# Attention heads: the 16 meta keys kept as 96 stacked rows, and one product in place of three

## The chip, the core and the metric

The kernel runs on one core of a Trainium2 chip. The metric is the device time of one execution in microseconds; the median of several runs counts. TensorE (PE) multiplies and transposes, VectorE (DVE) and ScalarE (ACT) do everything element by element, SyncE (SP) issues the loads. Each engine works through its own instructions in a fixed order and waits on the others by semaphores.

## The reference, cut to what matters

512 frames with 16 learned meta tokens ahead of them (528 rows of 1024) pass through two layers. Layer 0 has two kinds of attention side by side, four differential heads and eight forgetting ("fox") heads; layer 1 is multi-scale retention. An MLP follows each. For every attention head, scores become probabilities, and the probabilities are multiplied by the values:

```
p_a = softmax(where(chunk_vis, s_a, -inf))
p_diff = p_a[:, :, 0] - lam * p_a[:, :, 1]
o_a = einsum('bhqk,bhkd->bhqd', p_diff, va)      # 4 heads, 128 value columns
...
p_b = softmax(where(frame_vis, s_b, -inf))
o_b = einsum('bhqk,bhkd->bhqd', p_b, vb)         # 8 heads, 64 value columns
```

The sum over k runs over 16 meta keys and 512 frame keys. The change is in how the 16 meta keys enter that sum. All of it is float32.

## The kernel before

**Products in three passes.** A float32 operand is split in a high part `h` (ACT rounds it into the format that TensorE takes at full rate) and a low part `l` (DVE: source minus `h`). A product is three matmuls, `h*h + h*l + l*h`, in one PSUM bank. `split` makes such a pair from a bank. With only 16 rows to sum over, a matmul still streams all its 512 columns, three times.

**Stacked rows.** The same three terms can be summed over rows instead. `split_stack` gets a bank with 96 rows, six copies of 16 rows, and makes one tile in which one pair of the copies holds the low part and the others the high part. If the other operand has high and low parts in matching rows, one matmul over 96 rows gives all three terms. Layer 1 does so already: there `hm`, the six-fold copy of the meta rows of the hidden state, makes the values' meta block as 96 rows, and `mix_values` has a branch for it.

**A head of attention in layer 0.** The loop runs over four differential heads and then over eight fox heads. For head h the code issues, in this order:

- `diff_scores` or `fox_scores`: for four blocks of 128 query rows the scores (PSUM tile `s_ps`), with bias and minimum on DVE and the exponential on ACT, into the probability tiles `e`. Between the blocks stand the "filler" matmuls (PSUM tile `mm` for the next head's projections, `v_ps` for the fox heads' values).
- `diff_mix` or `fox_mix` of the head before (PSUM tile `o_ps`): `mix_values` multiplies values by probabilities in 12 matmuls over frame keys and three over the 16 meta keys.
- the scores between the meta rows themselves (`sm_ps`).
- `turn`: the probabilities are transposed on TensorE (PSUM tiles `t_ps`). Ten transposes of 128x128 fill three banks, four transposes of the 16 meta columns (`e[:, :16]`) a fourth. ACT and DVE split the banks: two of them at once into `turned` (in the last two heads one by one), the half-filled third and the meta bank into pairs `s`.

**The meta rows as queries** are few enough for one softmax over many heads: `meta_turn` transposes those 16x16 probabilities (`mt_ps`), `diff_meta_mix` and `fox_meta_mix` multiply them (`mo_ps`), three matmuls of 16 columns for each head.

**Order.** From the first head to the last, the flag `pe.on` chains every matmul and transpose to the one before it, so TensorE runs in the order of the code. ACT, DVE and the queue SP are put in order by the compiler's scheduler when the kernel is built. Tiles called `s`, `st`, `copies`, `e` and `turned` come from one pool of 43 buffers in SBUF, `s_ps`, `o_ps`, `v_ps` and the single `t_ps` from four PSUM banks, `mm` and the double `t_ps` from two pairs of banks.

Nearly all matmuls are recorded under line 156 and all transposes under line 159 (the helper that keeps the order), `split` under 352 (ACT) and 353 (DVE), `split_stack` under 416 and 418, the weights' split under 228 and 229.

Of the kernel before, what the change touches and what calls it, by code (L numbers as in the profile page):

```python
# [14 lines left out]
P = 128  # L15
# [3 lines left out]
META = 16  # L19
# [102 lines left out]
def kernel(  # L122
# [51 lines left out]
    def two(dt=F32, name="u"):  # L174
        t = both(dt, name)
        return t[:, 0, :], t[:, 1, :]
# [16 lines left out]
    def f(t):  # L193
        return t.bitcast(F32)
# [182 lines left out]
    for j in range(KT // 2):  # L377
        raw = both(F32, "xf")
        for i in range(2):
            load(raw[:, i, :], x[2 * j + i])  # L380
        for i in range(2):
            pair = both(F32R, "s")
            xs.append(split(raw[:, i, :], dst=(pair[:, 0, :], pair[:, 1, :])))
            act.copy(out=hm[:, 2 * j + i, :4 * META].rearrange("p (a c n) -> p a c n", a=2, c=2),
                     in_=f(pair)[:, :, :META].rearrange("p a (o n) -> p a o n", o=1).broadcast_to([P, 2, 2, META]))
        if j < 3:
            prepare(load)

# [25 lines left out]
    def split_stack(src, low, n):  # L414
        t = two(F32R, "st")[0]
        act.copy(out=t[:STACK, :n], in_=src)
        rows = slice(32 * low, 32 * low + 32)
        dve.tensor_tensor(out=t[rows, :n], in0=src[rows, :], in1=f(t)[rows, :n], op=ALU.subtract)
        return t
# [11 lines left out]
    def value_split(ps, t, n):  # L431
        if t < 4:
            return split(ps, n=512)
        if n == STACK:
            return split_stack(ps[:n, :], 2, 512)
        s = two(F32, "vm")[0][:32, :512]
        act.copy(out=s, in_=ps[32:64, :])
        dve.tensor_tensor(out=s, in0=s, in1=ps[:32, :], op=ALU.add)
        return split(s[:META], rows=slice(0, META), n=512)

    def value_block(xs, wts, t, n=4 * META):
        ps = bank("v_ps")
        for k in range(KT):
            for i in range(3 if t < 4 else 2):
                value_part(ps, xs, k, t, wts[k // 2], n, i)
        return value_split(ps, t, n)

    def value_streamed(xs):
        accs = [bank("v_ps") for _ in range(4)] + [two_banks("vm_ps")[:, 0, :]]
        for k in range(KT):  # L450
            if k % 2 == 0:
                wt = weights("B", ahead=3)
            order = [(t, i) for t in range(5) for i in range(3 if t < 4 else 2)]
            for t, i in order:
                value_part(accs[t], xs, k, t, wt, 4 * META, i)
        return [value_split(accs[t], t, 4 * META) for t in range(5)]

    va = value_streamed(xs)
    load_constants()
# [95 lines left out]
    def meta_scores(q, k, rows, fox, slot, into):  # L555
# [6 lines left out]
            pe.matmul(ps[:META, :META], lhsT=lhs, rhs=rhs, start=j == 0, stop=j == len(ops) - 1)  # L562
        dve.tensor_tensor(out=into[:, slot % 8, :], in0=ps[:META, :META], in1=mb_sb[:, slot, :], op=ALU.add)

    def turn(ps_list, wide=True):
        banks = [[(0, i) for i in range(4)], [(1, 1), (1, 2), (1, 3), (3, 3)], [(2, 2), (2, 3)]]

        def flip(ps, blocks):
            for c, (j, i) in enumerate(blocks):
                pe.transpose(out=ps[:, P * c:P * c + P], in_=ps_list[i][:, META + P * j:META + P * j + P],  # L570
                             identity=ident)
        turned = []
        if wide:
            ps = two_banks("t_ps")
            h, l = (both(F32R, "turned")[:, :, :512] for _ in range(2))
            for b in range(2):
                flip(ps[:, b, :], banks[b])
            act.copy(out=h, in_=ps)
            dve.tensor_tensor(out=l, in0=ps, in1=f(h), op=ALU.subtract)
            turned = [(h[:, b, :], l[:, b, :]) for b in range(2)]  # L580
        for blocks in banks[len(turned):]:
            ps = bank("t_ps")
            flip(ps, blocks)
            turned.append(split(ps, n=P * len(blocks)))
        ps = bank("t_ps")
        for i in range(4):
            pe.transpose(out=ps[:META, P * i:P * i + P], in_=ps_list[i][:, :META], identity=ident)
        turned.append(split(ps[:META, :512], rows=slice(0, META), n=512))
        return turned

    def mix_values(turned, v, vc0, ps):
        spans = [(0, 0, P, 0, 512, 0), (1, 1, P, 0, 384, 128), (2, 2, P, 0, 256, 256), (1, 3, P, 384, 128, 384),
                 (3, 4, META, 0, 512, 0)]
        stacked = not isinstance(v[4], tuple)
        if stacked:
            spans = spans[:4]
        for s, (src, blk, rows, s0, n, o0) in enumerate(spans):
            for i, (a, b) in enumerate(PASSES):
                pe.matmul(ps[:, o0:o0 + n], lhsT=v[blk][a][:rows, vc0:vc0 + P], rhs=turned[src][b][:rows, s0:s0 + n],
                          start=s == 0 and i == 0, stop=s == 4 and i == 2)  # L600
        if stacked:
            pe.matmul(ps, lhsT=v[4][:STACK, vc0:vc0 + P], rhs=turned[3][:STACK, :512], start=False, stop=True)

    os_ = [None] * KT
    od_t = [both(F32, "od") for _ in range(2)]
# [43 lines left out]

    def meta_turn(p, n):  # L650
        ps = bank("mt_ps")
        for i in range(n):
            pe.transpose(out=ps[:META, META * i:META * i + META], in_=p[:, i, :], identity=ident[:META, :META])
        return split(ps[:META, :META * n], rows=slice(0, META), n=META * n)

    def diff_meta_probs():
        meta_softmax(sm_d, 8)
# [6 lines left out]
    def diff_meta_mix(pt):  # L664
        ps = bank("mo_ps")
        for h in range(4):
            for i, (a, b) in enumerate(PASSES):
                pe.matmul(ps[:, META * h:META * h + META], lhsT=va[4][a][:META, P * h:P * h + P],
                          rhs=pt[b][:META, META * h:META * h + META], start=i == 0, stop=i == 2)
        for j in range(2):  # L670
            act.copy(out=od_t[j][:, :, :META],
                     in_=ps[:, 2 * META * j:2 * META * j + 2 * META].rearrange("p (a b) -> p a b", a=2))
# [95 lines left out]
    def fox_meta_mix(h0, h1, pt):  # L768
        ps = bank("mo_ps")
        for h in range(h0, h1):  # L770
            c = META * (h - h0)
            for i, (a, b) in enumerate(PASSES):
                pe.matmul(ps[:, c:c + META], lhsT=vb[4][a][:META, P * (h // 2):P * (h // 2) + P],
                          rhs=pt[b][:META, c:c + META], start=i == 0, stop=i == 2)
        for h in range(h0, h1):
            rows = slice(64 * (h % 2), 64 * (h % 2) + 64)
            dh, dl = os_[4 + h // 2]
            src = ps[rows, META * (h - h0):META * (h - h0) + META]
            act.copy(out=dh[rows, :META], in_=src)
            dve.tensor_tensor(out=dl[rows, :META], in0=src, in1=f(dh)[rows, :META], op=ALU.subtract)  # L780
# [490 lines left out]
    def ret_start(norm):  # L1271
        dst = [two(F32R, "qk") for _ in range(4)]
        aw = [weights("A") for _ in range(4)]
        bw = [weights("B") for _ in range(4)]
        v = [None] * 5

        for t in range(4):
            span = (META, HALF - META) if t < 2 else H1
            split_span(early_highs(aw[t], hs, span, None if t else norm), span, dst=dst[t])
        step(norm)  # L1280
        v[0] = value_block(hs, bw, 0, STACK)
        v[4] = value_block(hs, bw, 4, STACK)
        step(norm)
        for t in range(4):
            split_span(early_highs(aw[t], hs, H2), H2, dst=dst[t])
        return dst[:2], dst[2:], v, bw
# [83 lines left out]
    for h in range(RET_HEADS):  # L1370
        if h:
            bw = [weights("B") for _ in range(4)]
            v = [None] * 5
        for t in range(5):
            if t == 2:
                turned = ret_scores(q, k, *consts)
            if v[t] is None:
                v[t] = value_block(hs, bw, t, STACK)
        bw = None
        outs = ret_values(turned, v)  # L1380
        turned = v = None
        ys += ret_gate(*outs)
        outs = None
        if h + 1 < RET_HEADS:
            consts = ret_consts(h + 1)
            q, k = ret_qk()
        if h % 2:
            jobs = out_jobs(ys, ALPHA if h == 1 else None)
            ys = []
            if h == 1:  # L1390
                for get, run in jobs:
                    run(get(), S_FULL)
            else:
                ht, h2 = new_hidden()
                norm = tail(jobs, S_FULL, S1, S2, lambda span, t=ht: layer_norm(span, 2, t))
# [91 lines left out]
```

## Time and profile before

| what | us |
|---|---|
| median of 3 runs (1514.15, 1514.27, 1518.35) | 1514.27 |
| the profiled execution, its own time | 1520.3 |
| its span, first to last instruction | 1518.4 |
| PE busy, share of the span | 1486.5, 98% |
| DVE busy | 893.7, 59% |
| ACT busy | 659.6, 43% |
| mean granted TensorE clock | 0.99 |

The time outside the span is 1.9 us. All durations that the prediction uses are from the one profiled execution, which took 6.0 us longer than the median of the runs. Attention in layer 0 lies between about 48 us (the first head's scores) and 307 us (the last head's meta rows) of the span. In the rows, a line such as `o_ps<-s 16*128 16x512` names the tile that is written, the tiles that are read, and then rows x columns: 16 rows are summed over, 128 rows come out, 512 columns are streamed.

### The profile page before, as it was taken

The numbers are of one execution on the slowest core, as the hardware profiler recorded it, in microseconds if no ns is written. First come the engines' busy times: TensorE is split into PE (matmuls) and PEld (weight loads), VectorE is DVE, ScalarE is ACT, GpSimd is POOL, SyncE is SP. The second block draws the span as 40 slices with busy tenths as digits, with TensorE's granted clock in tenths as the row PEclk, the third lists the DMA queues.
The fourth block names the chain that finished last, engine by engine and source line by source line (L and its number), as shares of the span: only waits on it lengthen the run. The fifth ranks groups of instructions, "written<-read, shape, count | busy, mean of one in ns | idle before, by whom it ended". The sixth has DMA issues, their size and how long they took to land.

```text
span 1518.4 us, 23221 instructions
## 1 busy us (share of the span) xinstructions
PE 1486.5 (98%) x9752; PEld 1337.6 (88%) x9752; DVE 893.7 (59%) x1498; ACT 659.6 (43%) x1020; POOL 0.2 (0%) x4
## 2 busy tenths in 40 slices
PE   8999999999999999999999999999999999999997
PEld 6887878799999999998888888888899889898986
DVE  4574466577847566558544355254368838566567
ACT  4474444435516335255444343153445516445342
POOL 0000000000000000000000000000000000000000
PEclk9999999899999999999999999999999999999998
DMA  7111102040313314244013035023150313414221
GB/s 244 51 48 56 57 29 86 29 153 15 112 56 98 126 56 140 57 128 135 29 42 124 27 109 167 1 70 109 42 181 29 107 43 114 126 56 139 72 82 56
DMA packets 39592, 129.02 MB, mean 85 GB/s; under 512 B 4724, under 2 KB 7172, under 8 KB 39488
## 3 DMA queue, kind: packets, MB, share of 16 engines
q1 hardware_dynamic: 39488, 127.54, 26.4%
q8 instruction: 76, 1.25, 0.3%
q14 instruction: 28, 0.23, 0.1%
HBM read 125.43 MB, written 2.10 MB: 84 GB/s over the span
## 4 chain that ended last, share of the span: by engine, by line
PE 91%; DVE 4%; DMA 2%; ACT 2%; issue 1%; ACTq 0%; DVEq 0%
PE bank L156 33%; PE mm L156 20%; PE v_ps L156 10%; PE qc L156 7%; PE s_ps L156 5%; PE o_ps L156 5%; PE qa L156 4%; DMA raw<-in_w 2%; PE qb L156 2%; PE qd L156 2%; PE t_ps L159 1%; DVE wl L229 1%; PE sum_ps L156 1%; ACT wh L228 1%; DVE y L956 1%
## 5 line engine op out<-in xcount | busy, mean ns | idle before, releaser
L229 DVE TENSOR_TENSOR wl<-raw,wh 128x1024 fp32r<-128x1024 f32 x200 | 242.1, 1220 | 75.0 <-ACT wh L228 72.0
L228 ACT CAST wh<-raw 128x1024 fp32r<-128x1024 f32 x200 | 205.9, 1046 | 112.1 <-DMA raw<-in_w 81.4
L156 PE MATMUL bank<-g,wh 128*128 128x512 f32 (+2 forms) x800 | 201.2, 342 | 1.0 <-ACT wh L228 1.0
L156 PEld LDWEIGHTS bank<-g,wh 128*128 128x128 f32 x800 | 137.3, 188 | 20.0 <-ACT wh L228 2.1
L156 PE MATMUL bank<-hh,wh 128*128 128x512 f32 (+3 forms) x448 | 145.6, 340 | 0.0
L156 PE MATMUL bank<-hh,wl 128*128 128x512 f32 (+3 forms) x448 | 141.4, 332 | 0.0
L156 PE MATMUL bank<-g,wl 128*128 128x512 f32 (+2 forms) x400 | 136.1, 341 | 0.0
L156 PE MATMUL mm<-g,wh 128*128 128x264 f32 x832 | 135.3, 285 | 0.5 <-ACT wh L228 0.5
L156 PE MATMUL bank<-hl,wh 128*128 128x512 f32 (+3 forms) x448 | 120.6, 331 | 4.3 <-DVE hl L948 4.3
L156 PEld LDWEIGHTS mm<-g,wh 128*128 128x128 f32 x832 | 115.3, 189 | 0.7 <-ACT wh L228 0.7
L156 PE MATMUL qc<-tc,wh 128*128 128x264 f32 (+1 forms) x576 | 106.3, 283 | 3.1 <-DVE up L1176 3.1
L156 PE MATMUL mm<-s,wh 128*128 128x264 f32 x544 | 94.7, 297 | 0.5 <-DVE s L362 0.5
L156 PEld LDWEIGHTS bank<-hh,wh 128*128 128x128 f32 x448 | 85.1, 190 | 10.4 <-ACT hh L960 1.2
L156 PEld LDWEIGHTS bank<-hh,wl 128*128 128x128 f32 x448 | 84.8, 190 | 8.5
L156 PEld LDWEIGHTS qc<-tc,wh 128*128 128x128 f32 x576 | 88.9, 188 | 3.7 <-DVE up L1176 3.5
L156 PEld LDWEIGHTS bank<-hl,wh 128*128 128x128 f32 x448 | 72.8, 189 | 14.0 <-DVE hl L948 4.9
L156 PE MATMUL mm<-g,wl 128*128 128x264 f32 x416 | 84.6, 285 | 0.0
L156 PEld LDWEIGHTS bank<-g,wl 128*128 128x128 f32 x400 | 75.2, 188 | 9.3 <-DVE wl L229 0.2
L156 PEld LDWEIGHTS mm<-s,wh 128*128 128x128 f32 x544 | 76.6, 192 | 6.9 <-issue 2.4
L156 PE MATMUL qc<-tc,wl 128*128 128x264 f32 (+1 forms) x288 | 81.8, 284 | 0.0
L228 ACT CAST wh<-sums 128x1024 fp32r<-128x1024 f32 x48 | 50.2, 1046 | 62.4 <-DVE sums L242 37.8
L229 DVE TENSOR_TENSOR wl<-sums,wh 128x1024 fp32r<-128x1024 f32 x48 | 58.6, 1221 | 24.0 <-PE mm L156 10.2
(315 smaller groups left out, 3128.3 us busy)
## 6 DMA issues: line engine op xcount, KB each, us to landing
raw<-in_w SPq DMA_DIRECT2D x224, 512.0 KB, 4.0
xf<-in_x SPq DMA_DIRECT2D x8, 264.0 KB, 5.6
y<-in_x SPq DMA_DIRECT2D x8, 264.0 KB, 4.3
out<-y SPq DMA_DIRECT2D x8, 256.0 KB, 2.2
nb<-in_c_nb SPq DMA_DIRECT2D x4, 264.0 KB
rd<-in_c_rd SPq DMA_DIRECT2D x4, 256.0 KB
rd<-in_c_rm SPq DMA_DIRECT2D x4, 192.0 KB, 4.3
fm<-in_c_fm SPq DMA_DIRECT2D x1, 264.0 KB, 2.9
```

What stands on the lines that cost most here:

```text
L156: return self.put(nc.tensor.matmul(*a, **k))
L159: return self.put(nc.tensor.transpose(*a, **k))
L228: act.copy(out=wh, in_=raw)
L229: dve.tensor_tensor(out=wl, in0=raw, in1=f(wh), op=ALU.subtract)
L956: dve.tensor_tensor(out=t, in0=t, in1=r, op=ALU.mult)
```

## The change

In layer 0 as in layer 1, the values' meta block is made as 96 rows from the six-fold `hm`, and split by `split_stack`. In `turn` and `meta_turn`, ACT first writes six copies of the 16 meta columns of each probability block into a tile `copies` (128x96, four of them side by side), and TensorE transposes these, so that the bank has 96 rows; `split_stack` splits it. `mix_values`, `diff_meta_mix` and `fox_meta_mix` then have one matmul over 96 rows where they had three over 16.

```diff
@@ loading x @@
-            act.copy(out=hm[:, 2 * j + i, :4 * META].rearrange("p (a c n) -> p a c n", a=2, c=2),
-                     in_=f(pair)[:, :, :META].rearrange("p a (o n) -> p a o n", o=1).broadcast_to([P, 2, 2, META]))
+            act.copy(out=hm[:, 2 * j + i, :].rearrange("p (c a n) -> p a c n", c=3, a=2),
+                     in_=f(pair)[:, :, :META].rearrange("p a (o n) -> p a o n", o=1).broadcast_to([P, 2, 3, META]))
@@ value_split @@
-        if n == STACK:
-            return split_stack(ps[:n, :], 2, 512)
-        s = two(F32, "vm")[0][:32, :512]
-        act.copy(out=s, in_=ps[32:64, :])
-        dve.tensor_tensor(out=s, in0=s, in1=ps[:32, :], op=ALU.add)
-        return split(s[:META], rows=slice(0, META), n=512)
+        return split_stack(ps[:n, :], 2, 512)
@@ turn @@
+    def stacked(t):
+        return t.rearrange("p (o n) -> p o n", o=1).broadcast_to([t.shape[0], STACK // META, META])
...
         ps = bank("t_ps")
+        copies = two(F32, "copies")[0]
         for i in range(4):
-            pe.transpose(out=ps[:META, P * i:P * i + P], in_=ps_list[i][:, :META], identity=ident)
-        turned.append(split(ps[:META, :512], rows=slice(0, META), n=512))
+            c = copies[:, STACK * i:STACK * i + STACK]
+            act.copy(out=c.rearrange("p (o n) -> p o n", n=META), in_=stacked(ps_list[i][:, :META]))
+            pe.transpose(out=ps[:STACK, P * i:P * i + P], in_=c, identity=ident)
+        turned.append(split_stack(ps[:STACK, :512], 1, 512))
@@ mix_values @@
-        spans = [(0, 0, P, 0, 512, 0), (1, 1, P, 0, 384, 128), (2, 2, P, 0, 256, 256), (1, 3, P, 384, 128, 384),
-                 (3, 4, META, 0, 512, 0)]
...
+        spans = [(0, 0, P, 0, 512, 0), (1, 1, P, 0, 384, 128), (2, 2, P, 0, 256, 256), (1, 3, P, 384, 128, 384)]
...
+        pe.matmul(ps, lhsT=v[4][:STACK, vc0:vc0 + P], rhs=turned[3][:STACK, :512], start=False, stop=True)
@@ meta_turn @@
+        copies = two(F32, "copies")[0]
         for i in range(n):
-            pe.transpose(out=ps[:META, META * i:META * i + META], in_=p[:, i, :], identity=ident[:META, :META])
-        return split(ps[:META, :META * n], rows=slice(0, META), n=META * n)
+            c = copies[:META, STACK * i:STACK * i + STACK]
+            act.copy(out=c.rearrange("p (o n) -> p o n", n=META), in_=stacked(p[:, i, :]))
+            pe.transpose(out=ps[:STACK, META * i:META * i + META], in_=c, identity=ident[:META, :META])
+        return split_stack(ps[:STACK, :META * n], 1, META * n)
@@ diff_meta_mix (fox_meta_mix in the same way, with vb) @@
-            for i, (a, b) in enumerate(PASSES):
-                pe.matmul(ps[:, META * h:META * h + META], lhsT=va[4][a][:META, P * h:P * h + P],
-                          rhs=pt[b][:META, META * h:META * h + META], start=i == 0, stop=i == 2)
+            pe.matmul(ps[:, META * h:META * h + META], lhsT=va[4][:STACK, P * h:P * h + P],
+                      rhs=pt[:STACK, META * h:META * h + META], start=True, stop=True)
```

How the instructions stand on the engines shows at three places. The first is TensorE at the end of the second fox head (h = 1), where the mix of head 0 ends, `turn` follows, and then come the first scores of the next head. Before:

```order
L156 MATMUL o_ps<-s 128x512 x3
L159 MATMUL t_ps<-ident,e 128x128 x10
L159 MATMUL t_ps<-ident,e 16x128 x4
L156 MATMUL s_ps<-s 128x144 x3
L156 MATMUL s_ps<-rows 128x144
```

The same place now:

```order
L156 MATMUL o_ps<-st 128x512
L159 MATMUL t_ps<-ident,e 128x128 x10
L159 MATMUL t_ps<-ident,copies 96x128 x4
L156 MATMUL s_ps<-s 128x144 x3
L156 MATMUL s_ps<-rows 128x144
```

Two of three matmuls over the meta keys are gone, and the last four transposes read `copies` and no longer `e`; nothing else of TensorE has moved there.

The second is ACT at the same place: its work after the scores of that head, from the split of a projection (`s<-mm`) over the mix's result (`o<-o_ps`) and the split of the `t_ps` banks to the next weights (`wh<-raw`). Before:

```order
L358 ACTIVATE s<-mm 128x528
L760 CAST o<-o_ps 64x512
L578 CAST turned<-t_ps 128x2x512
L352 CAST s<-t_ps 128x256
L352 CAST s<-t_ps 16x512
L228 CAST wh<-raw 128x1024
```

Now:

```order
L358 ACTIVATE s<-mm 128x528
L758 CAST o<-o_ps 64x512
L576 CAST turned<-t_ps 128x2x512
L352 CAST s<-t_ps 128x256
L587 COPY copies<-e 128x96 x4
L416 CAST st<-t_ps 96x512
L228 CAST wh<-raw 128x1024
```

The scheduler has put the four copies behind the casts of the three banks that the first ten transposes fill, and ahead of the cast of the meta bank. In all ten heads with the wide `turned` the copies stand behind that cast and the 128x256 cast; in the last two they stand behind three casts.

The third is ACT at the `meta_turn` of the differential heads, between two projections (`s<-mm`) whose matmuls stand on TensorE directly before and behind the transposes into `mt_ps`. Before:

```order
L352 CAST s<-vm 16x512
L228 CAST wh<-raw 128x1024
L358 ACTIVATE s<-mm 128x528
L352 CAST s<-mt_ps 16x64
L228 CAST wh<-raw 128x1024
```

Now:

```order
L416 CAST st<-v_ps 96x512
L228 CAST wh<-raw 128x1024
L358 ACTIVATE s<-mm 128x528
L651 COPY copies<-pm 16x96 x4
L416 CAST st<-mt_ps 96x64
L228 CAST wh<-raw 128x1024
```

Here the copies have come behind the split of the projection that ends just ahead of the transposes.

More of the change, by code (lines that the diff above doesn't have):

```diff
@@ L433, in value_split, with value_block @@
             return split(ps, n=512)
-        if n == STACK:
-            return split_stack(ps[:n, :], 2, 512)
-        s = two(F32, "vm")[0][:32, :512]
-        act.copy(out=s, in_=ps[32:64, :])
-        dve.tensor_tensor(out=s, in0=s, in1=ps[:32, :], op=ALU.add)
-        return split(s[:META], rows=slice(0, META), n=512)
-    def value_block(xs, wts, t, n=4 * META):
+        return split_stack(ps[:n, :], 2, 512)
+    def value_block(xs, wts, t, n=STACK):
         ps = bank("v_ps")
@@ L454, in value_streamed @@
             for t, i in order:
-                value_part(accs[t], xs, k, t, wt, 4 * META, i)
-        return [value_split(accs[t], t, 4 * META) for t in range(5)]
+                value_part(accs[t], xs, k, t, wt, STACK, i)
+        return [value_split(accs[t], t, STACK) for t in range(5)]
     va = value_streamed(xs)
@@ L585, in turn @@
         ps = bank("t_ps")
+        copies = two(F32, "copies")[0]
         for i in range(4):
-            pe.transpose(out=ps[:META, P * i:P * i + P], in_=ps_list[i][:, :META], identity=ident)
-        turned.append(split(ps[:META, :512], rows=slice(0, META), n=512))
+            c = copies[:, STACK * i:STACK * i + STACK]
+            act.copy(out=c.rearrange("p (o n) -> p o n", n=META), in_=stacked(ps_list[i][:, :META]))
+            pe.transpose(out=ps[:STACK, P * i:P * i + P], in_=c, identity=ident)
+        turned.append(split_stack(ps[:STACK, :512], 1, 512))
         return turned
     def mix_values(turned, v, vc0, ps):
-        spans = [(0, 0, P, 0, 512, 0), (1, 1, P, 0, 384, 128), (2, 2, P, 0, 256, 256), (1, 3, P, 384, 128, 384),
-                 (3, 4, META, 0, 512, 0)]
-        stacked = not isinstance(v[4], tuple)
-        if stacked:
-            spans = spans[:4]
+        spans = [(0, 0, P, 0, 512, 0), (1, 1, P, 0, 384, 128), (2, 2, P, 0, 256, 256), (1, 3, P, 384, 128, 384)]
         for s, (src, blk, rows, s0, n, o0) in enumerate(spans):
@@ L599, in mix_values @@
                 pe.matmul(ps[:, o0:o0 + n], lhsT=v[blk][a][:rows, vc0:vc0 + P], rhs=turned[src][b][:rows, s0:s0 + n],
-                          start=s == 0 and i == 0, stop=s == 4 and i == 2)
-        if stacked:
-            pe.matmul(ps, lhsT=v[4][:STACK, vc0:vc0 + P], rhs=turned[3][:STACK, :512], start=False, stop=True)
+                          start=s == 0 and i == 0, stop=False)
+        pe.matmul(ps, lhsT=v[4][:STACK, vc0:vc0 + P], rhs=turned[3][:STACK, :512], start=False, stop=True)
     os_ = [None] * KT
@@ L771, in fox_meta_mix @@
             c = META * (h - h0)
-            for i, (a, b) in enumerate(PASSES):
-                pe.matmul(ps[:, c:c + META], lhsT=vb[4][a][:META, P * (h // 2):P * (h // 2) + P],
-                          rhs=pt[b][:META, c:c + META], start=i == 0, stop=i == 2)
+            pe.matmul(ps[:, c:c + META], lhsT=vb[4][:STACK, P * (h // 2):P * (h // 2) + P],
+                      rhs=pt[:STACK, c:c + META], start=True, stop=True)
         for h in range(h0, h1):
@@ L1280, in ret_start @@
         step(norm)
-        v[0] = value_block(hs, bw, 0, STACK)
-        v[4] = value_block(hs, bw, 4, STACK)
+        v[0] = value_block(hs, bw, 0)
+        v[4] = value_block(hs, bw, 4)
         step(norm)
@@ L1377 @@
             if v[t] is None:
-                v[t] = value_block(hs, bw, t, STACK)
+                v[t] = value_block(hs, bw, t)
         bw = None
```

## The prediction

> **What bounds the kernel now.** I read the engines' busy shares first, then the busy time by stretch for attention in layer 0 (the only place that changes), then the timeline around one `turn`, and last the granted clock. The shares (engine, busy us, share of the span, instructions):
>
> ```profile
> PE 1486.5 (98%) x9752; PEld 1337.6 (88%) x9752; DVE 893.7 (59%) x1498; ACT 659.6 (43%) x1020; POOL 0.2 (0%) x4
> ```
>
> The second view has, for each stretch, its length, the busy time of PE, of its weight loads, of DVE, ACT and POOL, and then the granted clock, the DMA share and GB/s:
>
> ```profile
> 48.00:313.00 265.00, 261.81 (x1707) 218.00 (x1707) 160.19 (x457) 128.42 (x277) 0.00 (x0) 0.97 0.17 56
> ```
>
> TensorE is idle for 265.00 - 261.81 = 3.2 us of all attention. ACT is busy for less than half of it. So TensorE is the bound, and ACT counts only where TensorE has to wait for it: whatever is taken from TensorE is gained, and whatever makes it wait is lost, with at most 3.2 us of older waits to hide in. The timeline at the end of fox head 1 (start, duration, engine, operation, count, and in brackets the idle time before and its releaser):
>
> ```profile
> 195.58 0.95 PE L156 MATMUL o_ps<-s 16*128 16x512 f32 x3
> ...
> 196.46 1.75 PE L159 MATMUL t_ps<-ident,e 128*128 128x128 f32 x14
> 196.56 0.58 ACT L760 CAST o<-o_ps 64x512 fp32r<-64x512 f32 x1 [2.59 <-PE o_ps L156]
> 197.64 1.01 ACT L578 CAST turned<-t_ps 128x1024 fp32r<-128x1024 f32 x1 [0.50 <-PE t_ps L159]
> ...
> 198.13 0.55 PE L156 MATMUL s_ps<-s 64*128 64x144 f32 x3
> 198.55 0.83 ACT L352 CAST s<-t_ps 128x256 fp32r<-128x256 f32 x2
> ```
>
> TensorE issues all 14 transposes in a row from 196.46 and goes on with the next head's scores at 198.13. ACT starts the cast of the wide `turned` only at 197.64, when eight transposes have ended, and comes to the 128x256 cast at 198.55: by then TensorE has been past the turn for 0.4 us. Nothing waits for ACT here.
>
> **What is taken off TensorE.** Matmuls of 512 columns follow each other at 0.23 us (780.01 to 780.24 here, in the timeline):
>
> ```profile
> 775.96 0.45 PE L156 MATMUL o_ps<-st 96*128 96x512 f32 x1
> ...
> 780.01 0.39 PE L156 MATMUL bank<-hh,wh 128*128 128x512 f32 x1
> 780.24 0.39 PE L156 MATMUL bank<-hl,wh 128*128 128x512 f32 x1
> ```
>
> The 96-row product that layer 1 already has takes 0.45 us against 0.39, and the three of 16 rows at 195.58 together 0.95, which is two steps of 0.23 and one duration; so I put the 96-row product at one of the three. Each of the 12 heads loses two matmuls: 12 x 2 x 0.23 = 5.5 us. The meta rows' mix, in the chain of waits (start, time on the chain, count), three times 12 matmuls (the last time one of them stands apart):
>
> ```profile
> 167.48 1.24 PE mo_ps L156 x12
> ...
> 264.68 1.24 PE mo_ps L156 x12
> 265.91 2.09 PE t_ps L159 x14
> ...
> 269.25 2.94 PE mm L156 x12
> ...
> 278.07 1.67 PE mm L156 x12
> ...
> 306.22 1.32 PE mo_ps L156 x11
> ```
>
> Four in place of 12 save 1.24 x 8/12 = 0.83, three times 2.5 us. Together **8.0 us off TensorE**. The transposes stream 128 columns as before and load 96 weight columns rather than 16; loads lie beside matmuls (1338 us of them do already), and I cost that at nothing. So too the values' block from 96 columns of `hm` (the same 512 streamed columns), the wider casts of `hm` while loading, and `value_split`, which loses a copy and an addition, under projections that run without a pause. No DMA is added, and SP's order is unchanged.
>
> **What is put in TensorE's way.** Four transposes now wait for ACT's copies. The order shows where these stand on ACT: behind the `turned` cast and behind the 128x256 cast, both of which wait for transposes of the same turn. TensorE's order is chained, so the next head's scores, projections and everything after them are queued behind the last of the four. The price of a copy is known from layer 1, where ACT writes the same six-fold copies (operation, duration ns min/median/max):
>
> ```profile
> L952 ACT CAST hm<-hh x4: 259/260/262, 714.2 to 718.6; 128x96 fp32r<-128x96 f32 x4
> ...
> L352 ACT CAST s<-t_ps x28: 346/569/593, 70.1 to 301.6; 128x256 fp32r<-128x256 f32 x12, 16x512 fp32r<-16x512 f32 x12, 128x512 fp32r<-128x512 f32 x4
> ```
>
> A copy is 0.26 us, the 128x256 cast (the shortest form in its row) 0.35 to 0.37. ACT starts an instruction about 0.1 before the last one ends (197.64 + 1.01 = 198.65, the next at 198.55), so four copies take 4 x 0.16 + 0.1 = 0.74. From the turn above: the cast starts at 198.55 and ends at 198.92; the copies run from 198.82 to 199.56; the last transpose follows some 0.05 later and the scores 0.1 behind it, at 199.7 instead of 198.13: **1.55 us of waiting per turn**. Were the copies to overlap with nothing, it would be 0.3 more; were they half the price, 0.3 less. These are the bounds, 1.25 to 1.85.
>
> Six turns are like this one: 9.3 us. In three, another ACT instruction lies between the two casts:
>
> ```profile
> 69.54 0.64 ACT L492 ACTIVATE fz<-fz 8x528 f32<-8x528 f32 x1
> ...
> 149.32 0.30 ACT L645 ACTIVATE sm_d<-sm_d 16x128 f32<-16x128 f32 x1
> ...
> 218.33 0.63 ACT L711 CAST rh<-r 36x528 fp32r<-36x528 f32 x1
> ```
>
> The first adds 0.55 after overlap, so 2.1; the other two turns come to 1.75, and 2.2 since L711 doesn't overlap with the cast ahead of it: 6.05 us. At the third turn TensorE waits already:
>
> ```profile
> 116.70 0.68 PE L156 MATMUL v_ps<-wh,s 128*128 128x512 f32 x1 [1.54 <-DVE s L353]
> ```
>
> The copies hide in those 1.54 us, and I take 0.3. The last two turns have a longer ACT chain but more waiting now (chain of waits, then ACT's timeline):
>
> ```profile
> 284.71 0.59 ACT o L760
> ...
> 286.80 0.81 PE s_ps L156 x4
> ```
>
> ```profile
> 285.32 2.03 ACT L352 CAST s<-t_ps 128x512 fp32r<-128x512 f32 x4
> ```
>
> Behind the cast `o`, ACT has four bank casts in 2.03; without the last (0.58, less 0.1 of overlap) the third ends near 286.7, and the copies end at 286.7 - 0.1 + 0.74 = 287.3, with the scores at 287.5 in place of 286.80: 0.75. In the last one `meta_turn` follows, and its copies stand behind the `st` cast: 1.6. The differential heads' `meta_turn` finally:
>
> ```profile
> 158.45 0.26 PE L159 MATMUL mt_ps<-ident,pm 16*16 16x16 f32 x4
> 158.56 0.61 ACT L358 ACTIVATE s<-mm 128x528 fp32r<-128x528 f32 x1 [2.90 <-PE mm L156]
> ```
>
> Its copies wait for that split to end (159.17) and take 0.74, so the transposes end at about 159.9 instead of 158.6: 1.35. In the fox heads' first `meta_turn` the copies stand ahead of the mix's cast and are done in time. Sum: 9.3 + 6.05 + 0.3 + 0.75 + 1.6 + 1.35 = **19.4 us of waiting**, 15.5 to 23 by the bounds. Against 8.0 us that is **11.4 us slower**, before the clock is counted.
>
> **The clock.** In attention the granted clock is halved in three places, each just behind a stretch in which TensorE streams little (columns as above, clock third from the end):
>
> ```profile
> 113.40:116.90 3.50, 1.96 (x19) 1.54 (x18) 2.80 (x4) 2.89 (x6) 0.00 (x0) 0.99 0.70 217
> 116.90:120.30 3.40, 3.40 (x9) 2.63 (x9) 3.06 (x7) 1.33 (x4) 0.00 (x0) 0.50 0.41 120
> 263.60:267.00 3.40, 3.40 (x28) 3.15 (x28) 2.07 (x6) 0.94 (x4) 0.00 (x0) 1.00 0.06 24
> 267.00:277.30 10.30, 10.30 (x40) 8.51 (x38) 4.46 (x11) 4.11 (x10) 0.00 (x0) 0.50 0.17 51
> 304.60:308.00 3.40, 3.40 (x26) 3.05 (x25) 3.02 (x4) 1.28 (x3) 0.00 (x0) 1.00 0.63 227
> 308.00:311.40 3.40, 3.40 (x18) 3.40 (x18) 1.67 (x3) 2.53 (x5) 0.00 (x0) 0.50 0.69 245
> ```
>
> The first follows 1.5 us of idling. The second follows the meta mix (1.24 us for 12 matmuls of 16 columns, which count as busy and stream next to nothing) and transposes, with no idle time; the third is like it. The halved stretches are one, three and one times 3.4 us, and their starts lie whole multiples of 3.41 apart (150.1 and 41.0), as if the clock were decided once in 3.4 us. At half clock 12 projections take 2.94 us, at full 1.67, so one such stretch costs 3.4 x (1 - 1.67/2.94) = 1.47, and the five in this profile 7.3 us. After the change each turn has 1.5 us and more without a matmul, between transposes and scores that fill half of the rows: as little as ahead of 117 and of 267. A pause of 1.55 lies whole in one 3.4 us stretch with a chance of (3.41 - 1.55)/3.41 = 0.55, and part of it may be enough. I take two in three of the 13 places, eight or nine drops, two of them of more than one stretch: 10 stretches, 14.7 us. The two drops behind the meta mixes should mostly go, since four matmuls are left there. Clock: 14.7 - 7.3 = 7.4 us more; the ends are 2 stretches (4.4 us less) and 25 (29 us more, if the clock stays half through a head's scores as at 267).
>
> The Trainium skill, page "TensorE: Matmul & The Clock Gate", section "Why this matters for your kernels", asks for "No PE-idle gaps >~3µs between matmul bursts"; by that rule, pauses of 1.6 us would cost nothing in clock, and the sum would be that of rival B. The trace does not agree: it shows the drop at 267 behind 3.40 us with no gap, and that at 117 behind a gap of half that length. The page's section on transposes says that these don't count as busy; that fits both.
>
> **The sum** against the profiled execution: 1520.3 + 11.4 + 7.4 = 1539. The median of the runs is 6.0 below that execution, and its slowest run 2.0 below; what varies is, I think, the number of halved stretches, which I count anew, so I take off only the 2.0: **1537 us**, 1.5% over 1514.27.
>
> **Rivals.** A is this forecast. B: the waits come, but the clock drops no oftener than before: 1514.3 + 11.4 = 1526, and 1522 with the short copies. For it: in the timed runs the clock cannot have cost much more than in the profile, though every turn has 1.7 us of transposes. C: the clock stays half through most heads, as it did for 10.3 us at 267: 25 stretches, 1520.3 + 11.4 + 29 = 1561. For it: scores stream 64 rows, which is little to wake it. D, on the other side: the copies don't hold TensorE up, because ACT reaches them before the tenth transpose has ended; then only the 8.0 us are left, 1506. It decides where a turn's wait is under 8.0/13 = 0.6 us. Against it: the `turned` cast alone ends 0.5 us after the scores began. E: no change, within 4.5 us, where the waits come out near 8 us, half of what I have; no row gives that.
>
> **Chances.** A 0.64, B 0.16, C 0.11, E 0.05, D 0.04. Measurements of this kernel tell 0.3% (4.5 us) from no change. Slower 0.91, the same 0.05, faster 0.04. The range goes from B's lower end, 1521, to just below C, 1558.
>
> **What would show it.** Right: TensorE idle ahead of `t_ps<-ident,copies` for about 1.0 to 1.6 us with ACT's copies as releaser, near 19 us in all; copies of 0.26 us behind the 128x256 cast; `o_ps<-st` once per head; a granted clock of 0.9 or less over attention, with drops just behind turns. Wrong: the wait ahead of the copies' transposes under 0.6 us, or a clock that stays at 1.0 behind turns (then B), or TensorE's older waits (3.2 us) taking up far more than I allow.

## The result, and the profile after

The changed kernel takes 1535.45 us (median of four runs, 1529.96 to 1542.97), the kernel before, beside it, 1516.15 (1514.15 to 1518.35). The ratio is 1.0133, with a 95% interval from 1.0105 to 1.0161: slower, by about 19 us. The profiled execution took 1535.16 us, with a span of 1533.4. The shares of its engines:

```profile
PE 1483.4 (97%) x9704; PEld 1335.3 (87%) x9704; DVE 896.1 (58%) x1496; ACT 670.3 (44%) x1078; POOL 0.2 (0%) x4
```

TensorE has 48 matmuls less, ACT 10.7 us of work more, which is still 44%. The time from 48 to 330 us (length, busy PE, PE's loads, DVE, ACT, POOL, and clock, DMA share, GB/s) holds attention of layer 0 and the projections behind it; in the kernel before, the layer's first row sums follow there (331.6 us), in the changed kernel only at 349.2:

```profile
48.00:330.00 282.00, 259.15 (x1664) 215.92 (x1665) 161.58 (x453) 138.35 (x336) 0.00 (x0) 0.96 0.16 51
```

The same 282 us of the kernel before, which get through more of the work:

```profile
48.00:330.00 282.00, 278.81 (x1846) 235.00 (x1846) 171.31 (x473) 132.63 (x281) 0.00 (x0) 0.97 0.20 65
```

TensorE's idle time in it has grown from 3.2 to 22.9 us. The five longest waits of the changed kernel (engine, tile and line that waited, for whom, us in total, times, longest) say for what:

```profile
PE t_ps L159 <- ACT copies L587: 17.3, 12, 1.9
PE mt_ps L159 <- ACT copies L651: 1.7, 2, 0.8
PE mm L156 <- ACT o L776: 1.2, 1, 1.2
PE s_ps L156 <- DVE low L540: 1.1, 3, 0.8
PE mm L156 <- DVE s L362: 1.1, 1, 1.1
```

All 12 turns wait for ACT's copies, and two of the three `meta_turn`. The lines of PE and ACT in the timeline of the turn that the prediction worked out, at the end of fox head 1:

```profile
203.58 0.45 PE L156 MATMUL o_ps<-st 96*128 96x512 f32 x1
203.86 1.25 PE L159 MATMUL t_ps<-ident,e 128*128 128x128 f32 x10
204.12 0.58 ACT L758 CAST o<-o_ps 64x512 fp32r<-64x512 f32 x1 [2.06 <-PE o_ps L156]
204.94 1.01 ACT L576 CAST turned<-t_ps 128x1024 fp32r<-128x1024 f32 x1 [0.24 <-PE t_ps L159]
205.84 0.38 ACT L352 CAST s<-t_ps 128x256 fp32r<-128x256 f32 x1
206.11 0.80 ACT L587 COPY copies<-e 128x96 f32<-128x96 f32 x4
206.45 0.83 PE L159 MATMUL t_ps<-ident,copies 128*96 128x128 f32 x4 [1.33 <-ACT copies L587]
207.20 0.55 PE L156 MATMUL s_ps<-s 64*128 64x144 f32 x3
```

The tenth transpose ends at 205.1. ACT is still in the `turned` cast, then does the 128x256 cast, and only then the copies, 206.11 to 206.91. TensorE waits 1.33 us for the first one, and then goes at the copies' pace: its last four transposes take 0.83 us. The scores, which began 1.67 us after the first transpose before, now begin 3.34 us after it. The clock was halved behind turns; two of the four places (stretch ahead, and the halved one):

```profile
186.20:189.60 3.40, 2.07 (x14) 1.42 (x12) 1.73 (x4) 2.74 (x8) 0.00 (x0) 0.99 0.00 0
189.60:193.00 3.40, 3.40 (x15) 3.16 (x15) 2.07 (x4) 1.26 (x3) 0.00 (x0) 0.50 0.08 19
227.00:230.40 3.40, 2.22 (x14) 1.80 (x15) 3.05 (x5) 3.00 (x9) 0.00 (x0) 1.00 0.00 0
230.40:237.30 6.90, 6.90 (x28) 5.84 (x26) 2.36 (x7) 1.30 (x5) 0.00 (x0) 0.51 0.23 80
```

In this execution six stretches of 3.4 us in attention are halved (the 0.96 of the stretch above: 282 x 0.04 x 2 / 3.41 is 6 to 7), five in the profile before. The timed runs differ in it: the one of 1529.96 has a mean clock of 0.990 and that of 1542.97 has 0.982, with 0.989 for the two between them (1535.16, which is the profiled one, and 1535.74).

### The profile page after: what moved, and what is told of

Its sections match the earlier page's. It is cut to its first block, busy times and chain, and to the rows that moved or that the text cites. A ratio compares the mean times of both kernels' runs of the same rounds, so it can differ in the third digit from the quotient of the medians.

```text
span 1533.4 us, 23182 instructions
## 1 busy us (share of the span) xinstructions
PE 1483.4 (97%) x9704; PEld 1335.3 (87%) x9704; DVE 896.1 (58%) x1496; ACT 670.3 (44%) x1078; POOL 0.2 (0%) x4
## 4 chain that ended last, share of the span: by engine, by line
PE 90%; DVE 4%; ACT 3%; DMA 2%; issue 1%; ACTq 0%; DVEq 0%
PE bank L156 34%; PE mm L156 20%; PE v_ps L156 10%; PE qc L156 6%; PE s_ps L156 4%; PE qa L156 4%; PE o_ps L156 4%; PE qb L156 2%; PE qd L156 2%; DMA raw<-in_w 2%; PE t_ps L159 1%; DVE wl L229 1%; PE sum_ps L156 1%; ACT wh L228 1%; DVE y L953 0%
```

## The experiments

The theory, W: TensorE waits for copies that stand too far back in ACT's queue; the waits outweigh the saved matmuls, and they also bring halved clock. Rivals: L, ACT has too much work around a turn, wherever the copies stand; K, most of the loss is halved clock that the change of products brings about by itself, and not the waits.

### The copies ahead of the casts

```diff
 def turn(ps_list, wide):
+    copies = two(F32, "copies")[0]
+    cs = [copies[:, STACK * i:STACK * i + STACK] for i in range(4)]
+    for i, c in enumerate(cs):
+        last = act.copy(out=c..., in_=stacked(ps_list[i][:, :META]))
...
-            act.copy(out=h, in_=ps)
+            cast = act.copy(out=h, in_=ps)
+            after(cast, last)          # order on ACT only, no wait
...
-    pm = diff_meta_probs()
+    pm = meta_copies(diff_meta_probs(), 4)
```

> The changed kernel with ACT's copies put ahead of the turned cast (in the last two heads ahead of the first bank cast), and the meta probabilities' copies made right behind their softmax. Theory W (TensorE waits for copies that stand behind casts): the waits ahead of the copies' transposes fall from 17.3 + 1.7 us to under 4 us in all, the two products saved per head remain, and the time is 6 to 10 us under the kernel before, about 1508. Rival L (ACT has too much work around a turn, wherever it stands): the wait moves to the casts and what reads them, and the time stays within 5 us of the changed kernel, 1530 to 1540. Rival K (most of the loss is the halved clock, which the change of products brings about by itself): 1520 to 1530, with five or more halved stretches in attention.

Measured 1505.99 us (1504.73 to 1507.92); ratio to the kernel before 0.9943, interval 0.9923 to 0.9963. The same instructions in another order on ACT turn 19 us of loss into 8 us of gain. TensorE's waits in attention, the four longest and the one for the copies:

```profile
PE t_ps L159 <- DVE o L773: 2.0, 2, 1.8
PE v_ps L156 <- DVE s L353: 1.7, 1, 1.7
PE t_ps L159 <- DVE e L626: 0.5, 1, 0.5
PE mm L156 <- DVE s L362: 0.5, 1, 0.5
...
PE t_ps L159 <- ACT copies L574: 0.3, 1, 0.3
```

Of 19.0 us for copies, 0.3 are left. What the copies delay instead, the casts, is waited for at length only once: 1.8 us in the last turn, where the meta copies have come ahead of the cast `o`. L is refuted: ACT's work is the same, 668.4 us in all. K too, since the products are the changed ones. This version beats both kernels.

### The copies on ACT, read by nobody

```diff
 # in the kernel before, behind the 128x256 cast
+    for i in range(4):
+        c = copies[:, STACK * i:STACK * i + STACK]...
+        after(act.copy(out=c, in_=same), cast)
     ps = bank("t_ps")
     for i in range(4):
         pe.transpose(out=ps[:META, ...], in_=ps_list[i][:, :META], identity=ident)
```

> The kernel before, with the 48 copies of the turns added on ACT at the place where the change has them, but read by nobody. Theory W: TensorE does not wait for them, so the time is that of the kernel before within 3 us. Rival L: ACT's 10 us of extra work, and the meta bank's cast that it delays by 0.7 us per turn, cost 6 us or more.

Measured 1516.76 us (1512.49 to 1521.97), ratio 1.0007, interval 0.9989 to 1.0025: no difference, to within 0.25%. ACT's extra work costs nothing that shows by itself. The profiled execution, the slowest of the ten, shows how much the clock can differ from one run to the next; behind the differential heads' meta mix the clock is halved for four stretches on end:

```profile
165.20:168.60 3.40, 3.40 (x26) 3.17 (x25) 1.93 (x2) 1.57 (x3) 0.00 (x0) 1.00 0.10 10
168.60:182.30 13.70, 13.70 (x50) 11.42 (x51) 3.40 (x12) 4.12 (x10) 0.00 (x0) 0.50 0.10 37
```

### The fewer products alone

```diff
 # in the kernel before; of the three products over 16 meta keys, high by high alone
+            passes = PASSES[:1] if s == 4 else PASSES
-            for i, (a, b) in enumerate(PASSES):
+            for i, (a, b) in enumerate(passes):
```

> The kernel before, with two of the three products over the 16 meta keys left out in each head and in the meta rows' mix (high by high alone remains), no copies. It shows what the fewer products are worth by themselves. Theory W: 8 to 10 us under the kernel before, of which 7.1 in the heads' mixes and 2.7 in the meta rows'. If the gain is under 4 us, part of it was cover for something else.

Measured 1505.18 us (1502.22 to 1508.43), ratio 0.9940, interval 0.9917 to 0.9964. The gain, 9 us beside a median of 1514.28, is in the range that was expected, but it is not all matmuls. The mix of a head, shown here for the same head as further below, takes 2.47 us:

```profile
192.13 2.47 PE o_ps L156 x13
```

Before it took 2.93, so two products fewer save 0.46 us per head, 5.5 us in 12 heads; with 2.7 in the meta rows' mixes that is 8.2 us. The clock has a part in the gain too: the run with a mean clock of 0.996 takes 1505.13 us, and the seven runs of the kernel before with that clock take 1511.56 to 1512.86, about 7 us more. The kernel with the copies ahead comes to nearly the same time, so it has kept nearly all of the gain.

### The wait filled with matmuls

```diff
 # in the changed kernel, behind the ten transposes
+        for _ in range(5):
+            pe.matmul(ps, lhsT=xs[0][0][:, :P], rhs=xs[0][0][:, :512], start=True, stop=True)
```

> The changed kernel with five matmuls of 512 columns put on TensorE between the tenth transpose of a turn and the four transposes of the copies; their result is overwritten by the transposes. They take about 1.15 us of the 1.33 us that TensorE waits there. Theory W: the length of the wait is ACT's, so it doesn't change, and what the matmuls alter is only the clock: no halved stretch behind a turn, and the time falls by what these cost, from 1535 to about 1527, with less spread between runs. If the halved clock is not caused by the waits, the time stays at 1535 and the halved stretches remain. If the waits are not what the trace says, the matmuls add their 13.8 us.

Measured 1524.40 us (1521.84 to 1524.98), ratio 1.0062, interval 1.0040 to 1.0084. Sixty more matmuls make the changed kernel 11 us faster, and its runs agree within 3 us instead of 13. TensorE is now busy for most of the turns, and the clock is up again:

```profile
48.00:330.00 282.00, 274.73 (x1801) 229.50 (x1800) 167.58 (x461) 141.43 (x340) 0.00 (x0) 0.99 0.19 58
```

The chain of waits of the same turn shows that the wait's own length has not changed:

```profile
203.37 0.89 PE t_ps L159 x8
...
205.19 0.38 ACT s L352
205.57 0.18 ACT copies L589
...
205.79 0.82 PE t_ps L159 x4
206.62 0.74 PE s_ps L156 x4
```

From the first transpose to the scores it is 206.62 - 203.37 = 3.25 us; in the changed kernel's chain it is 207.27 - 204.02 = 3.25. So of the 19 us about half is the waits less the saved matmuls (10 us over the kernel before remain), and the other half is what goes with TensorE having nothing to stream in them, the clock above all. That much of the loss is clock, as K has it, but it comes with the waits and not with the products. In the profiles, four of six halved stretches are gone, at most 4 x 1.7 = 6.8 us of the 9.8 by which the first row sums come earlier; waits on other engines, smaller by about 2 us, are most of the rest. The two halved stretches that are left, from 107.3 to 114.1 us, follow a wait of 1.0 us ahead of a projection and not a turn.

### Small and wide matmuls in the turns

Both start from the kernel with the copies ahead, and put matmuls at the same place, 12 of 16 rows and 16 columns, or five of 128 rows and 512 columns:

```diff
+        for _ in range(12):
+            pe.matmul(ps[:, :META], lhsT=xs[0][0][:META, :P], rhs=xs[0][0][:META, :META], start=True, stop=True)
```

> The kernel with the copies ahead (1506.0), and in each of the 12 turns 12 matmuls of 16 rows and 16 columns between the tenth transpose and the copies' transposes; the transposes overwrite what they write. TensorE has no idle time there, but streams next to nothing for about 1.2 us per turn, as behind the meta mixes of the kernel before. Theory G (the clock goes by what is streamed in 3.4 us, so such matmuls are as bad as waiting): 14 us for the matmuls and about 10 more for six or more halved stretches in attention, 1526 to 1534, with a wide spread. Rival I (the clock goes by idle time, and an engine that issues is not idle): 14 us alone, 1518 to 1522, at most two halved stretches in attention.

> The same with five matmuls of 512 columns in place of the 12 small ones: 5 x 0.23 = 1.15 us per turn. Theory G and rival I alike: 13.8 us for the matmuls and at most two halved stretches in attention, 1518 to 1522. Its difference to the small ones is the clock's share by theory G (about 10 us) and nothing by rival I.

Measured: small 1531.83 us (1525.64 to 1534.83), wide 1519.09 (1516.30 to 1521.16); the ratios to the kernel before are 1.0077 (1.0050 to 1.0104) and 1.0008 (0.9989 to 1.0027). The first row is of the small ones, the second of the wide ones:

```profile
48.00:330.00 282.00, 278.32 (x1790) 236.37 (x1791) 160.81 (x453) 136.62 (x333) 0.00 (x0) 0.93 0.16 51
```

```profile
48.00:330.00 282.00, 276.62 (x1848) 235.10 (x1847) 172.13 (x471) 142.90 (x340) 0.00 (x0) 0.99 0.20 63
```

With the small ones TensorE is idle for less time, 3.7 us against 5.4, and yet its clock is 0.93 against 0.99: twelve halved stretches against two. So the idle time that the profile counts is not what the clock goes by (rival I is refuted); it matters what the matmuls stream. Rows and columns were made small together, so which of the two counts stays open. The profile of the small ones is that of the slowest of five runs: its mean clock over the whole is 0.985, while the two fastest (1525.64, 1525.67) have 0.992 and 0.991. The price was not matched exactly. In the chain of the turn at fox head 1, first the small ones:

```profile
201.69 1.43 PE t_ps L156 x12
203.12 0.57 PE t_ps L159 x4
```

```profile
199.70 1.15 PE t_ps L156 x5
200.85 0.44 PE t_ps L159 x4
```

The small ones with the transposes behind them take 0.41 us more, 4.9 us in 12 turns; the other 7.8 us of the 12.7 between the medians are put down to the clock, by difference.

### The copies on GpSimd

```diff
 # in turn of the changed kernel, in code ahead of the ten transposes' banks
+    for i, c in enumerate(cs):
+        last = nc.gpsimd.tensor_copy(out=c..., in_=stacked(ps_list[i][:, :META]))
...
-            act.copy(out=c..., in_=stacked(ps_list[i][:, :META]))
```

> The changed kernel with the 48 copies of the turns on GpSimd, which has nothing else to do, instead of ACT; the meta probabilities' copies stay on ACT as changed. Theory W (it is the place in ACT's queue): the copies start when the probabilities are ready, and four of them, at up to 0.5 us each, end no later than 0.6 us behind the tenth transpose; waits there under 6 us in all and a time of 1505 to 1515. Rival L (too much ACT work) expects a gain here too, but not with the copies ahead on ACT, where it is already refuted; if GpSimd takes over 0.6 us for a copy, the waits come back and the time is near 1535.

Measured 1507.34 us (1506.33 to 1507.47), ratio 0.9923, interval 0.9908 to 0.9938: as good as with the copies ahead on ACT. A copy takes (duration ns min/median/max)

```profile
L574 POOL COPY copies<-e x48: 263/270/1295, 52.2 to 287.0; 128x96 f32<-128x96 f32 x48
```

and TensorE waits for none of them (the times of GpSimd are rough in these profiles). Of the waits for copies, what is left are those for the meta copies, which stayed on ACT:

```profile
PE mt_ps L159 <- ACT copies L661: 2.3, 2, 1.5
```

## Why the prediction was right, and where it was not

**The mechanism** was right. The copies stand where the order showed them, cost 0.28 us each where 0.26 was taken, and hold TensorE up in every turn; rival D had the copies start ahead of the tenth transpose's end, and they start 1.0 us behind it. The kernel with the copies ahead shows that the place alone does it.

**The saved matmuls** were put at 8.0 us; the chain of waits has 9.8. The mix of a head before and after the change, and the meta rows' mix after it (1.24 before):

```profile
193.60 2.93 PE o_ps L156 x15
```

```profile
201.68 2.35 PE o_ps L156 x13
...
173.27 0.34 PE mo_ps L156 x4
```

That is 0.58 here and 0.59 on average, where I had 2 x 0.23 = 0.46: 7.1 us in all, and 0.9 rather than 0.83 per meta mix, 2.7 us. The step of 0.23 was right for the two products that are gone, as the kernel with the fewer products shows (2.93 to 2.47). What I had wrong is the third: I put the 96-row product at one of the 16-row ones, and it takes 0.12 to 0.13 less (2.47 to 2.35 here). Why is not shown.

**The waits**, scores' delay included, were put at 19.4 us. Measured in the same way, from the first transpose of a turn to what follows it, the 12 turns and the differential heads' `meta_turn` are 21.7 us longer than before, with the 1.54 us taken off that TensorE waited behind the third turn. The ordinary turn has 1.67 to 1.82 where I had 1.55; the last two have 0.9 and 2.1 where I had 0.75 and 1.6. (In the first of these I had added up wrongly: 285.32 + 2.03 - 0.48 is 286.9 and not 286.7, which would have made it 0.9.)

**Other waits** grew by about 3.3 us; I had none. The largest is 1.2 us behind the last head, for the fox heads' meta rows.

**The clock** was the step that failed in size: ten halved stretches in attention and +7.4 us, and in the profile there are six, +1.5. The waits less the matmuls were 21.7 - 9.8 = 11.9 us, where I had 11.4, and with the other waits 15.2. With the clock's 1.5 that makes 16.7 of the 17.6 us by which the layer's first row sums come later in the profile (331.6 before, 349.2 after; 14.9 are left at the end), and the sum had 18.8. So the total came out near because the clock, put 6 us too high, stood in for other waits that I did not have, and because the copies' waits and the saved matmuls were each put about 2 us too low. That part was luck.

Against the medians it looks much the same. The profiled execution of the kernel before was 6.0 us slower than its median, and I took off only 2.0, so the forecast had 7.4 + 4.0 = 11.4 us of clock over the median. The two middle runs of the changed kernel (1535.16, 1535.74) have a mean clock of 0.989. The three timed runs of the kernel before with that clock, from the experiments, take 1521.52 to 1522.64, 12 to 14 us less. So of the 19.3 us between the medians, some 6 are the clock's, about half of what was forecast, and some 13 are the waits less the matmuls.

**The rule on gaps** of the Trainium skill (page "TensorE: Matmul & The Clock Gate", section "Why this matters for your kernels"), by which pauses of 1.3 us would have cost no clock and rival B been right, does not fit here if a gap is what the profile counts as idle: halved stretches follow turns with gaps of 1.1 to 1.9 us, and filling these gaps gains 11 us, most of it clock. What the same page of the Trainium skill says of PE-mode transposes, that they don't count as busy, was not tested by itself. It leaves another reading: between the last matmul of the mix and the next scores lie 3.2 us (204.03 to 207.20), which is about the length of the rule's gap. The small matmuls speak against that reading too, since they stand in the middle of such a stretch and the clock fell all the same, unless matmuls as small as these don't count either. No run here settles it.

## What to carry to other kernels

When an engine that has slack feeds a full one, its share of busy time says nothing: read where the new instruction stands in its queue, and what the instructions ahead of it wait for. Here four copies per turn, behind two casts, turned a gain into a loss of 19 us, and the same copies ahead of the casts, or on an idle engine, left the gain of 8. And a wait on TensorE, or a run of matmuls that stream a few columns, can cost more than its own length, by way of the clock: here, 19 us of waits for copies went with some 6 us of clock, and 17 us of small matmuls (12 x 1.43) with some 8. Fill the wait with wide matmuls to see how much of the time that is.

## What the runs showed of the hardware that I had not expected

Small matmuls can bring the clock down while TensorE counts as 99% busy (278.32 of 282 us, clock 0.93). Wide matmuls that do nothing useful made a kernel 11 us faster. At the end of a head's mix, a product over 96 rows takes 0.12 us less than one over 16 rows (2.35 against 2.47 us for 13 matmuls). GpSimd copies a 128x96 tile in a median of 270 ns, as fast as ACT (271 with the copies ahead), though one of 48 took 1295.
